# Stick-breaking attention: the softplus of the next key block is issued ahead of the sum of the present one

## The chip, the cores and the metric

The kernel runs on one core of one Trainium2 chip. The metric is the device time of one launch in microseconds (us), as the median of three runs. Engines are named as in the profile: PE is TensorE's matmul stream and PEld its weight loads, DVE is VectorE, ACT is ScalarE, POOL is GpSimd, and SP is the engine that issues most DMA transfers. Each engine takes its own instructions in the order in which they stand in its queue, and waits on semaphores for the others.

## The reference, cut to what matters

A decoder layer: an input projection, a chunked gating MLP beside stick-breaking attention (4 heads of 128, 1,024 positions), an output projection, and a mixture of 32 experts. Everything is float32. The change touches the attention alone:

```python
z = jnp.einsum('bhqd,bhkd->bhqk', qb, kf[:, :, :kl]) * scale
log_fail = jnp.where(causal, jax.nn.log_sigmoid(-z), 0.0)
within = jnp.einsum('bhqni,ij->bhqnj', log_fail, after_in_block)
later = lax.cumsum(blk, axis=3, reverse=True) - blk
log_a = jax.nn.log_sigmoid(z) + (within + later[..., None])
a = jnp.where(causal, jnp.exp(log_a), 0.0)
outs.append(jnp.einsum('bhqk,bhkd->bhqd', a, vt))
```

The key blocks of a query are swept from the last to the first, since the sum over later keys must be known before a block's weights can be formed.

## The kernel before

The attention works on key blocks of 128 (index j) against up to 512 queries at once. A `Chain` is one head and one half of the queries. Two chains of two heads run side by side, called c0 and c1 here, and a loop step k handles one key block of both. `seq` lists the 24 steps: two pairs of chains over the first half of the queries with 4 key blocks each (steps 0 to 3 and 4 to 7), and two pairs over the second half with 8 (steps 8 to 15 and 16 to 23). Because of causality the first key blocks of a pair touch 128, then 256, then 384 queries, and all others 512, so that every pair begins with widths 128, 256, 384, 512.

For one block and one head the stages are these. `z` (PE, L655) makes the scores, with a mask matmul (L659) on the diagonal. `e0`, `e1`, `e2` (ACT, L664, L669, L673) form ln(1 + exp(-|z|)) in the tile e. `sp` issues three instructions: the softplus sp = max(z, 0) + e (DVE, L681), its rounded part sh (DVE, a cast, L682), and its low part sl = sp - sh (POOL, L683). `ls` (DVE, L689) is min(z, 0) - e. `tri` (PE, L697 with sh and L698 with sl) adds the sum inside the block to the running PSUM tile cum. `add` (DVE, L702) forms ls + cum, `exp` (ACT, L713) the weights, and `av` (PE, L719) their product with the values. `comp` (PE, L708 and L709) then completes cum for the next block; it overwrites what `add` reads, so it waits for `add`.

The order is written out by hand under a manual schedule: each engine gets its instructions in the order of the loop's calls, and `each(k, f)` issues stage f for c0 and then c1. `z` and the three e stages run two steps ahead, `sp` and `ls` one step ahead. A finished pair is normalized by `fin0` to `fin5`: `fin0` in the next pair's first step, `fin1` to `fin3` in its second (PE L730, POOL L128, PE L736, DVE L740), `fin4` in its third and `fin5` (the DVE subtraction L748, called yl) in its fourth. After the attention come two transfers issued on POOL (L1076, into the tile xk that holds the keys before), and the output projection.

Of the kernel before, what the change touches and what calls it, by code (L numbers as in the profile page):

```python
# [58 lines left out]
def body(ctx, tc, A, out):  # L59
# [366 lines left out]
    def at(s, fn):  # L426
        todo.setdefault(s, []).append(fn)
# [192 lines left out]
    def wo_load(i):  # L620
        if i < 16:
            cg, b = i // 4, (i + 2) % 4
            wo_raw[i] = wr.tile([P, 2, 512], F32, name="wo")
            SY.dma_start(wo_raw[i], A["w_out"][cg, b])
# [8 lines left out]
    def ya_load(t):  # L633
        y = op.tile([P, DG], F32, name="yld")
        SY.dma_start(y, y_d[t * P:(t + 1) * P, :])
        return y

    with ExitStack() as c3:
# [113 lines left out]
        with tc.manual_schedule():  # L752
            seq = []
            for half in range(2):
                for hp2 in range(2):
                    ch = [Chain(half, 2 * hp2), Chain(half, 2 * hp2 + 1)]
                    seq += [(ch, j) for j in range((half + 1) * HT - 1, -1, -1)]
            n = len(seq)

            def each(i, f):  # L760
                if 0 <= i < n:
                    ch, j = seq[i]
                    for c in ch:
                        f(c, j)

            for i in range(2):
                wo_load(i)
            G.dma_start(wgr, A["w_gr"])
            yas = {t: ya_load(t) for t in range(2)}

            def scores(i):
                for f in (Chain.e0, Chain.e1, Chain.e2):
                    each(i, f)

            def first(i):
                return 0 <= i < n and seq[i][1] == seq[i][0][0].top

            each(0, Chain.z)
            each(1, Chain.z)
            scores(0)  # L780
            each(0, Chain.sp)
            each(0, Chain.ls)
            scores(1)
            for k in range(n + 1):
                each(k, Chain.tri)
                each(k, Chain.add)
                each(k + 2, Chain.z)
                each(k, Chain.comp)
                if 0 < k and seq[k - 1][1] == 0:
                    for i in range(6):  # L790
                        for c in seq[k - 1][0]:
                            at(k + (0, 1, 1, 1, 2, 3)[i], getattr(c, f"fin{i}"))
                if first(k - 2):
                    each(k - 2, Chain.av)
                if not first(k - 1):
                    each(k - 1, Chain.av)
                each(k + 1, Chain.sp)
                each(k + 1, Chain.ls)
                each(k + 2, Chain.e0)
                each(k, Chain.exp)  # L800
                each(k + 2, Chain.e1)
                each(k + 2, Chain.e2)
                for f in todo.pop(k, []) if k < n else ():
                    f()
            fins = [f for k in sorted(todo) for f in todo[k]]
            todo.clear()
# [710 lines left out]
```

## Time and profile before

| | |
|---|---|
| median of 3 runs | 1617.72 us (1617.65 to 1617.85) |
| profiled execution | 1615.23 us, of which span 1613.4 us |
| attention in the profiled execution | from 535.07 us (first z) to about 668 us of the span |
| mean granted TensorE clock | 0.973 of full speed |

The span is the time from the first to the last instruction of the profiled execution. The time of that execution is 1.8 us longer than its span and 2.5 us below the median of the runs, so differences are made against the execution's own time and then carried over to the median. Stretches of the trace are given as microseconds from the span's start.

### The profile page before, as it was taken

The numbers are of one execution on the slowest core, as the hardware profiler recorded it, in microseconds if no ns is written. First come the engines' busy times: TensorE is split into PE (matmuls) and PEld (weight loads), VectorE is DVE, ScalarE is ACT, GpSimd is POOL, SyncE is SP. The second block draws the span as 40 slices with busy tenths as digits, with TensorE's granted clock in tenths as the row PEclk, the third lists the DMA queues.
The fourth block names the chain that finished last, engine by engine and source line by source line (L and its number), as shares of the span: only waits on it lengthen the run. The fifth ranks groups of instructions, "written<-read, shape, count | busy, mean of one in ns | idle before, by whom it ended". The sixth has DMA issues, their size and how long they took to land.

```text
span 1613.4 us, 21346 instructions
## 1 busy us (share of the span) xinstructions
PE 1518.8 (94%) x6818; PEld 1151.6 (71%) x6818; DVE 1221.2 (76%) x2220; ACT 945.1 (59%) x2014; POOL 315.2 (20%) x288
## 2 busy tenths in 40 slices
PE   4999998999999899899999869999989999999996
PEld 4788887888888665578878656666656666666664
DVE  5889675867787588668856768887868888888883
ACT  5442588755434667432223467777767777777771
POOL 2000132010011334320001322324221212211111
PEclk8899999999999999999999979999989999999998
DMA  9987478768776000468857568999999999999972
GB/s 378 351 315 242 155 260 297 258 238 310 279 258 228 1 1 1 154 211 299 291 187 289 200 209 318 354 369 346 387 341 365 360 361 370 366 362 356 358 299 33
DMA packets 94394, 433.94 MB, mean 269 GB/s; under 512 B 13073, under 2 KB 13185, under 8 KB 64193
## 3 DMA queue, kind: packets, MB, share of 16 engines
q1 hardware_dynamic: 82000, 377.54, 63.3%
q0 software_dynamic: 11984, 52.85, 11.2%
q10 hardware_dynamic: 288, 2.10, 0.3%
q8 instruction: 56, 0.92, 0.2%
q14 instruction: 66, 0.53, 0.1%
HBM read 399.89 MB, written 43.02 MB: 275 GB/s over the span
## 4 chain that ended last, share of the span: by engine, by line
PE 40%; DMA 34%; issue 13%; DVE 5%; ACT 4%; POOL 2%; POOLq 0%; another core or an unknown queue 0%; SPq 0%; DVEq 0%; ACTq 0%
DMA out<-y,idx 22%; PE acc L322 22%; PE acc L867 9%; DMA xg<-u_d,idx 7%; DMA out<-xi 2%; DMA wm<-in_w_mod 2%; PE lg L913 1%; PE yp L719 1%; POOL sl L683 1%; PE z L655 1%; DVE macc L182 1%; DVE sp L681 1%; ACT junk L347 1%; DVE sh L682 1%; PE tr L906 1%
## 5 line engine op out<-in xcount | busy, mean ns | idle before, releaser
L1282 DVE TENSOR_TENSOR wl<-wx,wh 128x1024 fp32r<-128x1024 f32 x256 | 309.5, 1219 | 13.5 <-ACT wh L1281 12.5
L1281 ACT ACTIVATE wh<-wx 128x1024 fp32r<-128x1024 f32 x256 | 273.4, 1070 | 49.0 <-PE gu L1291 34.8
L1314 PE MATMUL dn<-wx,actT 128*128 128x512 f32 x512 | 242.4, 597 | 6.1 <-DMA wx<-in_w_down 5.5
L1291 PE MATMUL gu<-wh,xh 128*128 128x512 f32 x512 | 239.7, 468 | 0.0
L182 DVE SCALAR_TENSOR_TENSOR macc<-wm,sc_c,macc 128x512 f32<-128x512 f32 x296 | 222.2, 751 | 11.5 <-DMA wm<-in_w_mod 3.4
L322 PE MATMUL acc<-wh,hh 128*128 128x512 f32 x640 | 209.8, 398 | 3.4 <-ACT hh L278 1.8
L322 PE MATMUL acc<-wl,hh 128*128 128x512 f32 x640 | 206.7, 393 | 2.9 <-DVE wl L307 2.7
L322 PE MATMUL acc<-wh,hl 128*128 128x512 f32 x640 | 206.6, 393 | 0.4 <-DVE hl L279 0.4
L1291 PE MATMUL gu<-wl,xh 128*128 128x512 f32 x512 | 203.1, 397 | 0.1
L1291 PE MATMUL gu<-wh,xl 128*128 128x512 f32 x512 | 201.9, 394 | 0.0
L1224 POOL DMA_INDIRECT out<-y,idx x52 | 94.9, 1825 | 459.2 <-DVE y L1315 453.1
L1315 DVE TENSOR_TENSOR y<-dn,gate 128x512 f32<-128x512 f32 x128 | 88.5, 692 | 112.0 <-PE dn L1314 101.6
L867 PE MATMUL acc<-wo,yh 128*128 128x512 f32 x512 | 169.3, 412 | 0.0
L1270 ACT ACTIVATE xh<-tp,b2c 128x128 fp32r<-128x128 f32 x512 | 146.8, 383 | 17.8 <-PE tp L1265 17.7
L1314 PEld LDWEIGHTS dn<-wx,actT 128*128 128x128 f32 x512 | 96.5, 189 | 82.6 <-issue 63.1
L1272 DVE SCALAR_TENSOR_TENSOR xl<-tp,b2c,xh 128x128 fp32r<-128x128 f32 x512 | 143.5, 343 | 3.9 <-ACT xh L1270 3.9
L322 PEld LDWEIGHTS acc<-wl,hh 128*128 128x128 f32 x640 | 120.7, 189 | 30.0 <-DVE wl L307 5.0
L322 PEld LDWEIGHTS acc<-wh,hl 128*128 128x128 f32 x640 | 121.2, 189 | 26.9 <-DVE hl L279 1.1
L322 PEld LDWEIGHTS acc<-wh,hh 128*128 128x128 f32 x640 | 119.6, 190 | 27.6 <-ACT hh L278 1.9
L307 DVE TENSOR_TENSOR wl<-w,wh 128x1024 fp32r<-128x1024 f32 x80 | 97.6, 1221 | 34.2 <-ACT wh L306 34.1
L306 ACT ACTIVATE wh<-w 128x1024 fp32r<-128x1024 f32 x80 | 83.0, 1053 | 63.1 <-PE acc L322 51.6
L1291 PEld LDWEIGHTS gu<-wl,xh 128*128 128x128 f32 x512 | 97.4, 190 | 30.2 <-issue 15.1
(246 smaller groups left out, 2326.7 us busy)
## 6 DMA issues: line engine op xcount, KB each, us to landing
wx<-in_w_gu SPq DMA_DIRECT2D x128, 1024.0 KB
wm<-in_w_mod SPq DMA_DIRECT2D x160, 512.0 KB
wx<-in_w_down SPq DMA_DIRECT2D x64, 1024.0 KB
w<-in_w_in SPq DMA_DIRECT2D x80, 512.0 KB
x<-in_w_mod SPq DMA_DIRECT2D x16, 1024.0 KB
wo<-in_w_out SPq DMA_DIRECT2D x16, 512.0 KB
xi<-in_x SPq DMA_DIRECT2D x24, 256.0 KB
out<-xi SPq DMA_DIRECT2D x24, 256.0 KB
```

Source lines behind the costliest of these rows:

```text
L182: V.scalar_tensor_tensor(self.acc, t[:, j, :], sc, self.acc, op0=ALU.mult, op1=ALU.add)
L307: V.tensor_tensor(wl, w, wh.bitcast(F32), op=ALU.subtract)
L322: T.matmul(accs[t], a, b, start=(first and j == 0 and n == 0), stop=(last and j == 1 and n == 2))
L867: T.matmul(acc, y[a][:, c, ts_], w[b][:, c % 2, :], start=(n_ == 0 and i == 0), stop=(n_ == 7 and i == 2))
L1224: return G.indirect_dma_start(out=out, out_offset=bass.IndirectOffsetOnAxis(ap=idx, axis=0), in_=y, in_offset=None, bounds_check=S - 1, oo ...
L1270: SC.activation(xh[:, j, :], self.p[:, j, :], AF.Identity, bias=b2c[:, b * 4 + j:b * 4 + j + 1])
L1272: V.scalar_tensor_tensor(xl[:, j, :], self.p[:, j, :], b2c[:, b * 4 + j:b * 4 + j + 1], xh[:, j, :].bitcast(F32), op0=ALU.add, op1=ALU.sub ...
L1281: SC.activation(self.wh[q], w, AF.Copy)
L1282: low = lambda: V.tensor_tensor(self.wl[q], w, self.wh[q].bitcast(F32), op=ALU.subtract)
L1291: T.matmul(self.gu, a[c // 4][:, c % 4, :], b[q][:, k, :], start=(c == 0 and i == 0), stop=(c == 15 and i == 2))
L1314: T.matmul(d, self.aT[:, f, :], self.wd[f][:, cs], start=(f == 0), stop=(f == 1))
L1315: V.tensor_tensor(self.y[:, cs], d, gate2[:, cs], op=ALU.mult)
```

## The change

The call that issues `sp` of step k+1 moves from behind the `av` calls to between `tri` and `add` of step k. Nothing is added or removed.

```diff
             for k in range(n + 1):
                 each(k, Chain.tri)
+                each(k + 1, Chain.sp)
                 each(k, Chain.add)
                 each(k + 2, Chain.z)
                 each(k, Chain.comp)
...
                 if not first(k - 1):
                     each(k - 1, Chain.av)
-                each(k + 1, Chain.sp)
                 each(k + 1, Chain.ls)
                 each(k + 2, Chain.e0)
                 each(k, Chain.exp)
```

The order of PE, ACT and SP is the same as before. On DVE, in a full step of the last pair (512 queries wide; ls<-ls,cum is `add`, ls<-z,e is `ls`, yl is `fin5` of the pair before, - is before and + is now):

```order
 L748 TENSOR_TENSOR yl_4731<-u_5243,yh_4730 128x512
 L748 TENSOR_TENSOR yl_4731<-u_5247,yh_4730 128x512
+L681 SCALAR_TENSOR_TENSOR sp<-z,e 128x512
+L682 CAST sh<-sp 128x512
+L681 SCALAR_TENSOR_TENSOR sp<-z,e 128x512
+L682 CAST sh<-sp 128x512
 L702 TENSOR_TENSOR ls<-ls,cum 128x512 x2
-L681 SCALAR_TENSOR_TENSOR sp<-z,e 128x512
-L682 CAST sh<-sp 128x512
-L681 SCALAR_TENSOR_TENSOR sp<-z,e 128x512
-L682 CAST sh<-sp 128x512
 L689 SCALAR_TENSOR_TENSOR ls<-z,e 128x512 x2
```

The two softplus instructions and the two casts of the next step stood behind the two `add`; now they stand ahead of them.

On DVE, at the third step of a pair that follows another (384 wide; u is the output of the finished pair, L740 is its `fin3`):

```order
 L740 SCALAR_TENSOR_TENSOR u_5243<-u_5243,hcol,yp 128x512
 L740 SCALAR_TENSOR_TENSOR u_5247<-u_5247,hcol,yp 128x512
+L681 SCALAR_TENSOR_TENSOR sp<-z,e 128x512
+L682 CAST sh<-sp 128x512
+L681 SCALAR_TENSOR_TENSOR sp<-z,e 128x512
+L682 CAST sh<-sp 128x512
 L702 TENSOR_TENSOR ls<-ls,cum 128x384 x2
-L681 SCALAR_TENSOR_TENSOR sp<-z,e 128x512
-L682 CAST sh<-sp 128x512
-L681 SCALAR_TENSOR_TENSOR sp<-z,e 128x512
-L682 CAST sh<-sp 128x512
 L689 SCALAR_TENSOR_TENSOR ls<-z,e 128x512 x2
```

Here the `add` of the 384-wide block goes behind the four instructions of the 512-wide one, all of them behind `fin3`.

On POOL, at the end of the attention (sl is the low part, the DMA rows are the two transfers into the old key tile):

```order
-L683 TENSOR_TENSOR sl<-sp,sh 128x512 x6
-L1076 DMA xk<-mod_d 128x2048
-L683 TENSOR_TENSOR sl<-sp,sh 128x512 x2
-L1076 DMA xk<-mod_d 128x2048
+L683 TENSOR_TENSOR sl<-sp,sh 128x512 x8
+L1076 DMA xk<-mod_d 128x2048 x2
 L683 TENSOR_TENSOR sl<-sp,sh 128x512 x2
```

The first transfer stood ahead of the sl of step 22 and now stands behind it, beside the second.

## Rows read from the trace of the kernel before

**Rows 1.** Busy time in stretches (us: each engine's busy us, clock, DMA share, GB/s).

```profile
600.00:620.00 20.00, 17.71 (x59) 9.94 (x59) 19.13 (x30) 12.85 (x28) 8.98 (x7) 1.00 0.00 0
```

**Rows 2.** Waits in the attention, 535 to 668 us: total us, times, longest.

```profile
PE cum L698 <- POOL sl L683: 10.7, 17, 1.0
...
DVE ls L702 <- PE cum L698: 7.1, 17, 1.2
...
DVE sp L681 <- ACT e L673: 2.7, 2, 2.4
```

**Rows 3.** Timeline, DVE in a full step: start us, us, instruction, [idle before <-releaser].

```profile
607.62 0.67 DVE L702 TENSOR_TENSOR ls<-ls,cum 128x512 f32<-128x512 f32 x1
...
609.14 0.68 DVE L681 SCALAR_TENSOR_TENSOR sp<-z,e 128x512 f32<-128x512 f32 x1
...
610.92 1.11 DVE L682 CAST sh<-sp 128x512 fp32r<-128x512 f32 x1
...
611.96 1.27 DVE L689 SCALAR_TENSOR_TENSOR ls<-z,e 128x512 f32<-128x512 f32 x2
```

**Rows 4.** Timeline, ACT in the same full step.

```profile
606.23 1.14 ACT L673 ACTIVATE e<-e 128x512 f32<-128x512 f32 x2
...
610.75 1.14 ACT L713 ACTIVATE ls<-ls 128x512 f32<-128x512 f32 x2
...
612.83 1.14 ACT L673 ACTIVATE e<-e 128x512 f32<-128x512 f32 x2
```

**Rows 5.** Timeline, PE and POOL around the same full step.

```profile
601.41 0.50 PE L698 MATMUL cum<-sl,tri_r 128*128 128x512 f32 x1 [0.41 <-POOL sl L683]
...
608.00 0.50 PE L698 MATMUL cum<-sl,tri_r 128*128 128x512 f32 x1 [0.95 <-POOL sl L683]
...
609.66 0.80 PE L708 MATMUL cum<-sh,comp_r 128*128 128x512 f32 x1
...
612.20 1.29 POOL L683 TENSOR_TENSOR sl<-sp,sh 128x512 fp32r<-128x512 f32 x1 [0.45 <-DVE sh L682]
...
613.55 0.51 PE L698 MATMUL cum<-sl,tri_r 128*128 128x512 f32 x1
```

**Rows 6.** Timeline, a pair's first step (add 128, sp 256).

```profile
556.20 0.42 DVE L681 SCALAR_TENSOR_TENSOR sp<-z,e 128x256 f32<-128x256 f32 x1 [0.28 <-ACT e L673]
...
556.95 0.28 PE L708 MATMUL cum<-sh,comp_r 128*128 128x128 f32 x1
...
557.89 0.74 DVE L689 SCALAR_TENSOR_TENSOR ls<-z,e 128x256 f32<-128x256 f32 x2
```

**Rows 7.** Timeline, a pair's third step (add 384, sp 512), behind fin3.

```profile
567.67 0.75 DVE L740 SCALAR_TENSOR_TENSOR u<-u,hcol,yp 128x512 f32<-128x512 f32 x1 [0.89 <-PE yp L736]
...
569.74 0.39 PE L708 MATMUL cum<-sh,comp_r 128*128 128x384 f32 x1
...
571.62 0.58 PE L697 MATMUL cum<-sh,tri_r 128*128 128x512 f32 x1
...
573.72 0.50 PE L698 MATMUL cum<-sl,tri_r 128*128 128x512 f32 x1 [0.94 <-POOL sl L683]
```

**Rows 8.** Timeline, the first pair, steps 1 to 3.

```profile
542.67 0.93 ACT L673 ACTIVATE e<-e 128x384 f32<-128x384 f32 x2
...
546.49 0.54 DVE L702 TENSOR_TENSOR ls<-ls,cum 128x384 f32<-128x384 f32 x1
...
547.76 0.39 PE L708 MATMUL cum<-sh,comp_r 128*128 128x384 f32 x1
...
552.19 0.50 PE L698 MATMUL cum<-sl,tri_r 128*128 128x512 f32 x1 [0.95 <-POOL sl L683]
```

**Rows 9.** Busy time in two stretches behind the attention (columns as in Rows 1).

```profile
672.00:674.00 2.00, 0.00 (x0) 0.00 (x0) 1.00 (x1) 1.97 (x3) 0.00 (x0) 1.00 0.78 229
676.00:678.00 2.00, 2.00 (x9) 1.81 (x9) 1.37 (x3) 0.21 (x1) 0.38 (x1) 0.50 0.52 209
```

**Rows 10.** Timeline, DVE near the end, the cast of c1 of step 22.

```profile
655.26 1.82 DVE L682 CAST sh<-sp 128x512 fp32r<-128x512 f32 x1
```

## The prediction

> **What bounds the attention now.** I read three views. The busy time of a stretch of full steps [rows 1] shows PE at 17.71 and DVE at 19.13 of 20 us, and DMA at 0.00: both engines are nearly full, and no transfer goes on that a longer or shorter attention could hide. So a microsecond won or lost here should move all that follows by as much.
>
> The waits [rows 2] show what the change can aim at: PE waits 10.7 us for the low parts sl, and DVE 7.1 us for `tri`. They also show the other side: DVE has waited for the e stages only twice, 2.7 us in all.
>
> The timeline of a full step [rows 3 to 5] shows the ring that sets its period. From the last `tri` of one step (608.00) to that of the next (613.55) it is 5.55 us: the last low part lets `tri` run, then come the second `add`, two softplus and two casts on DVE, the low part of c1 on POOL (612.20, 1.29 long), and `tri` at 613.55. The change takes `add` out of this ring, and if nothing else closed, PE would not wait for sl any more.
>
> **What the move does.** DVE takes its instructions in order, so each `add` now waits until the four sp and sh instructions ahead of it are done. What waits for `add` is `comp` on PE, with `av` and the next `tri` queued behind it, and `exp` on ACT, with the e1 and e2 of step k+2 behind that. And e2 of step k+2 is what the next softplus waits for. A new ring closes, once around per step: exp(k), e1 and e2 (k+2), sp and sh (k+2), add(k+1), exp(k+1). Before, `add` stood ahead of the softplus, so the same dependences needed two steps per turn.
>
> In the trace the softplus has some room, but not enough. e2 of c0 is done at about 606.85 [rows 4] (606.23, and 0.62 for the first of the pair), and its softplus starts at 609.14 [rows 3], so it could go 2.3 us earlier. But softplus and casts take 609.14 to 611.96, 2.82 us. In this step `add` would start at 607.62 + 2.82 = 610.44 and end 0.67 later, at 611.1, while `comp` began at 609.66 [rows 5]: PE loses over 1 us at once.
>
> **A. Full steps.** The new ring from rows: exp to e2 2.08 us, 610.75 to 612.83 [rows 4], first e2 0.62 (four ACT instructions in 2.08 are 0.52 each, so of a pair's 1.14 the first needs 0.62), softplus and casts 2.82, `add` 0.67: 6.19. I take 6.2 with the handoffs, against 5.55. In the step that also holds yl, before 6.59, from 601.41 to 608.00 [rows 5], DVE is full in both orders: I take 6.65. In each second-half pair four steps follow a 512-wide one, one of them with yl: 3 x 0.65 + 0.06 = 2.0 us, for two pairs **+4.1**.
>
> **B. First step of a pair.** The softplus of 256 starts at 556.20, already behind a wait for e2, and its casts end at 557.89 [rows 6]. `add` of 128 then needs about 0.28 (0.67 and 0.54 for 512 and 384 [rows 3, 8], 0.13 less for each 128), so `comp` starts at 558.2 and not at 556.95. PE's queue stands 1.25 us. Three pairs follow another one in this way: **+3.8**.
>
> **C. Third step of a pair.** The second L740 ends at 568.42 [rows 7]; now 2.82 of softplus and casts and 0.54 of `add` come before `comp`, which starts at 571.78 and not at 569.74: 2.04 late. Behind it `tri` of the 512 block goes, whose last part waited 0.94 us for sl; that wait is now gone, which leaves 1.1. PE's ends are modelled, so this is an upper bound, and the lower is about 0.5 if the true wait was longer; I take 1.0. Three pairs: **+3.0**.
>
> **D. First pair.** No `fin3` stands there, so the ring itself decides. e2 of 384 is done for c0 at about 543.2 [rows 8]; softplus and casts of 384 lie halfway between 1.69 and 2.82 [rows 3, 6], 2.26, and `add` of 256 is 0.41: exp(1) at 545.9. From there exp 0.61 (ACT pairs of 256, by the steps between 0.93 and 1.14), e1 1.04, e2 0.62, softplus and casts 2.82 and `add` 0.54: `comp` of step 2 at 551.5 and not at 547.76. The way from `comp` to the last `tri` is that of C, 1.88 and 1.16 without its wait: 554.6 and not 552.19. **+2.2**, with the same caveat.
>
> **Clock.** In D PE stands still for 3.8 us. In 672 to 674 us PE did nothing, and at 676 to 678 the granted clock was 0.50, which is 1.2 of 2.4 GHz [rows 9]. Some 2.7 us of PE work (`comp`, `av`, `tri`) would then take twice as long; I count **+1.5** for the chance that the fall hits it whole.
>
> **E. End.** The cast of c1 in step 22 took 1.82 and not 1.11 [rows 3, 10], since the first transfer on POOL held up the low part of c0. The transfer now stands behind step 22: **-0.7**. Both transfers feed only the output projection behind the attention; if they came too late, its first use of the tile would wait.
>
> Nothing is added to any engine, so the costs are all order. Sum: 4.1 + 3.8 + 3.0 + 2.2 + 1.5 - 0.7 = **+13.9 us**. Against the profiled execution: 1615.2 + 13.9 = 1629.1. The median of the runs lies 2.5 above that execution, which gives **1631.6 us**, 0.9% slower.
>
> **Rivals.**
>
> *Faster: the new ring stays open.* If e2 were always done early enough, PE's 10.7 us of waiting for sl would go: 1617.7 - 10.7 = 1607.0. For it speaks that DVE hardly ever waited for e2 [rows 2]. It decides at `comp`: `add` must be done when z of step k+2 is through, so the softplus would have to move up by at least 2.82 us, and rows 3 and 4 show 2.3 of room in a step with wide blocks and none in a narrow one [rows 6]. Chance 0.07.
>
> *About even: the low parts pay for the sums.* PE's delays at `comp` and its waits at `tri` are in the same queue; if each delay took the place of a wait, the 10.7 us would be given back in full against the 13.9: +3.2, 1620.9. Against it: B has no wait for sl behind it to give back, and in A the ring does not go through sl. Chance 0.10, and half of that within the limit of no change.
>
> *Slower still: the clock falls in the new waits.* Each full step would have about 1 us of PE standing still, on top of the shorter gaps that it has. A full step at 1.2 GHz needs at least 10 us of PE: its matmuls fill about 5.3 of the 5.55 now. That is +4.4 us above 6.2 for each such step; three of them give about 1645. In 600 to 620 PE's gaps were no bar to a clock of 1.00 [rows 1], and the rows of 672 to 678 needed a gap of over 2 us. The Trainium skill (TensorE: Matmul & The Clock Gate, "HAM oscillation — how this bites in real kernels") says that bursts of matmuls with long waits between them bring the clock down again and again. By that rule the fall would come back in every step; [rows 9] agree for one long wait, and no row here shows it for short ones. Chance 0.13.
>
> **How the numbers follow.** My forecast has 0.70, with its own range 1624 to 1639: A could be +5.7 if PE's work behind `comp` adds to the ring, B to D could be half. The range of 8 in 10 reaches from 1621 (the even case) to 1643 (two or three slow-clock steps); it leaves out the faster case, the lowest even ones and the clock's tail. A change within 0.2% (3.2 us) can't be told from none here. Faster by more 0.07, within 0.07 (half the even case, the lowest of the forecast), slower 0.86.
>
> **What the profile after would show.** Right: a period of 6.2 us between the last `tri` of full steps; DVE's softplus waiting for ACT's e2 in most steps, far above 2.7 us in all; PE's wait for sl near zero, and in its place PE waiting for `add` (L702) at `comp`; the first pair's `comp` of step 2 near 551.5; the output projection beginning about 14 us later and all behind it as before. Wrong: a full step at 5.4 us or less, or `comp` that starts as soon as z is through. If the attention is longer by 14 us but the whole is not, a transfer behind it had room that I did not see.

## The result, and the profile after

The changed kernel took **1635.52 us** (median of 4 runs, 1633.39 to 1638.57) against 1617.78 us (1617.65 to 1617.90): a ratio of 1.0112, with an interval of 1.0097 to 1.0126. It is slower by 1.1%, or 17.7 us; the forecast was 13.9.

The profiled execution took 1634.69 us, with a span of 1632.8 us and a mean granted clock of 0.971. It is 19.5 us longer than the one of before. 0.7 of that lies ahead of the attention, 17.6 in it, and 1.2 behind it. The attention is measured here from the start of the last `tri` matmul (L698 of c1) of step 0 to that of step 23: 124.90 us before (539.18 to 664.08) and 142.46 after (539.86 to 682.32).

The waits of the attention, 535 to 690 us (engine, line, what it waited for: us in total, times, longest), beside [rows 2]:

```profile
PE cum L708 <- DVE ls L702: 24.3, 16, 2.6
...
ACT ls L713 <- DVE ls L702: 19.2, 15, 3.2
...
DVE sp L681 <- issue: 11.4, 8, 2.5
DVE sp L681 <- ACT e L673: 9.1, 8, 2.4
...
PE cum L698 <- POOL sl L683: 0.2, 1, 0.2
```

Read it from the bottom. The wait at which the change could aim, PE for the low parts, fell from 10.7 us to 0.2. In its place PE waits 24.3 us for `add` (L702) at `comp` (L708), ACT waits 19.2 for the same `add`, and the softplus (L681) waits 9.1 for e2. The 11.4 put down to "issue" end when e2 ends as well (the one before the softplus at 549.11 ends 0.70 after the e2 pair began at 548.41). That is a ring seen from its three engines: `add` waits for the softplus, `exp` for `add`, and the next softplus for the e2 behind `exp`.

The timeline of the full steps that answer to [rows 3 to 5] (start us, us, instruction, [idle before <-releaser]):

```profile
615.06 1.23 ACT L713 ACTIVATE ls<-ls 128x512 f32<-128x512 f32 x2 [0.54 <-DVE ls L702]
615.08 0.50 PE L708 MATMUL cum<-sh,comp_r 128*128 128x512 f32 x1 [1.20 <-DVE ls L702]
...
617.23 1.13 ACT L673 ACTIVATE e<-e 128x512 f32<-128x512 f32 x2
617.94 0.69 DVE L681 SCALAR_TENSOR_TENSOR sp<-z,e 128x512 f32<-128x512 f32 x1 [1.12 <-ACT e L673]
...
619.34 1.27 POOL L683 TENSOR_TENSOR sl<-sp,sh 128x512 fp32r<-128x512 f32 x1 [3.45 <-DVE sh L682]
...
619.87 1.02 DVE L682 CAST sh<-sp 128x512 fp32r<-128x512 f32 x1
620.81 1.27 DVE L702 TENSOR_TENSOR ls<-ls,cum 128x512 f32<-128x512 f32 x2
621.52 1.23 ACT L713 ACTIVATE ls<-ls 128x512 f32<-128x512 f32 x2
621.54 0.50 PE L708 MATMUL cum<-sh,comp_r 128*128 128x512 f32 x1 [0.76 <-DVE ls L702]
```

One turn of the ring goes from `exp` at 615.06 to `exp` at 621.52, 6.46 us: 2.17 from `exp` to e2 (617.23), 0.71 to the softplus (617.94), 2.87 for softplus and casts to `add` (620.81), 0.71 to the next `exp`. The steps before and behind are the same (608.59 to 615.06, 621.52 to 627.98). `comp` starts with the first `exp`, since both need the same `add`.

The busy time and the clock in stretches (columns as in [rows 1]):

```profile
546.00:558.00 12.00, 8.86 (x34) 7.70 (x35) 9.21 (x19) 5.17 (x14) 4.61 (x6) 0.72 0.00 1
572.00:576.00 4.00, 3.67 (x20) 3.52 (x19) 2.53 (x5) 0.56 (x2) 0.00 (x0) 0.68 0.00 0
578.00:582.00 4.00, 3.77 (x13) 3.54 (x14) 2.97 (x8) 2.83 (x8) 2.08 (x3) 0.57 0.00 0
605.00:625.00 20.00, 16.87 (x51) 8.74 (x50) 17.12 (x27) 15.00 (x27) 7.66 (x6) 1.00 0.00 0
628.00:634.00 6.00, 6.00 (x15) 3.32 (x16) 3.44 (x9) 2.01 (x6) 1.68 (x3) 0.72 0.00 1
678.00:682.00 4.00, 3.26 (x10) 1.87 (x11) 2.48 (x5) 1.23 (x2) 2.43 (x2) 1.00 0.47 181
```

In full steps (605 to 625) no engine is full any more: DVE fell from 19.13 of 20 us to 17.12. They wait for one another around the ring. PE stands still for up to 1.2 us in each step there, and the granted clock stays at 1.00. In the four stretches at 546 to 558, 572 to 582 and 628 to 634 it fell towards 0.50 (1.2 GHz). Before, the same four had 1.00; of the attention only 566 to 570 us (0.57, at the matmuls of `fin1` to `fin3`, which run at 572 to 576 after) and 586 to 590 us (0.59, and 1.00 after) were low.

PE at the places of terms D, C and A, at the last `comp` that waits for `add`, and at the first matmul of the output projection:

```profile
552.57 0.44 PE L708 MATMUL cum<-sh,comp_r 128*128 128x384 f32 x1 [2.40 <-DVE ls L702]
...
578.23 0.69 PE L708 MATMUL cum<-sh,comp_r 128*128 128x384 f32 x1 [2.56 <-DVE ls L702]
...
625.11 0.40 PE L698 MATMUL cum<-sl,tri_r 128*128 128x512 f32 x1
...
633.28 0.40 PE L698 MATMUL cum<-sl,tri_r 128*128 128x512 f32 x1
...
678.74 0.50 PE L708 MATMUL cum<-sh,comp_r 128*128 128x512 f32 x1 [2.48 <-DVE ls L702]
...
686.34 0.72 PE L867 MATMUL acc<-wo,yh 128*128 128x512 f32 x2
```

The output projection began at 668.20 before: it is 18.1 us later. The step from 625.11 to 633.28 is 8.17 us long where a full step has 6.46; the clock was at 0.72 in it (628 to 634). The wait of 2.48 us ahead of 678.74 is longer than most others, and the clock behind it stayed at 1.00 (678 to 682).

Set against each other by the same mark, the last `tri` of each step, the attention grew as follows:

| stretch (step to step) | before, us | after, us | longer by |
|---|---|---|---|
| D: first pair, 0 to 3 | 13.01 | 16.88 | 3.87 |
| B: first step of a pair, 4 to 5, 8 to 9, 16 to 17 | 4.25, 4.25, 4.20 | 5.64, 5.64, 5.22 | 3.8 (1.39, 1.39, 1.02) |
| C: third step, 6 to 7 | 5.41 | 7.81 | 2.40 (clock 0.57) |
| C: third steps, 10 to 11 and 18 to 19 | 5.50, 5.73 | 6.73, 6.72 | 2.2 |
| 9 to 10 | 9.33 (clock 0.59 at 586 to 590) | 7.53 | -1.80 |
| A: full steps 11 to 15 | 23.19 | 27.96 | 4.77 (clock 0.72 in the last) |
| A and E: full steps 19 to 23 | 23.87 | 26.27 | 2.40 |
| all others together | | | -0.1 |

### The profile page after: what moved, and what is told of

Same layout as the page of the kernel before. It is cut to its first block, busy times and chain, and to the rows that moved or that the text cites. A ratio compares the mean times of both kernels' runs of the same rounds, so it can differ in the third digit from the quotient of the medians.

```text
span 1632.8 us, 21326 instructions
## 1 busy us (share of the span) xinstructions
PE 1523.0 (93%) x6818; PEld 1154.2 (71%) x6818; DVE 1218.7 (75%) x2220; ACT 947.7 (58%) x2014; POOL 315.4 (19%) x288
## 4 chain that ended last, share of the span: by engine, by line
DMA 32%; PE 12%; issue 12%; DVE 2%; ACT 1%; POOLq 0%; POOL 0%; another core or an unknown queue 0%; DVEq 0%; ACTq 0%
DMA out<-y,idx 22%; PE acc L867 9%; DMA xg<-u_d,idx 7%; DMA out<-xi 2%; PE lg L913 1%; PE tr L906 1%; DVE sp L681 0%; DVE sh L682 0%; DVE wo L836 0%; DMA b2c<-mod_d 0%; ACT wo L835 0%; DVE xk L951 0%; DMA wo<-in_w_out 0%; ACT ls L713 0%; PE gu L1291 0%
```

## Experiments

The theory (T1) is the ring of the prediction: exp, e1 and e2, softplus and casts, `add`, once around per step. The rival (T2) is that `add` is late only because DVE has four more instructions ahead of it: then `comp` waits whatever ACT does, and the way over `exp` plays no part. The profiled execution of each kernel gives the steps; the kernel before had medians of 1617.58 us beside the first four kernels, 1616.88 beside the next four, and 1617.04 beside the last two. Ahead of the attention and behind it, where all these kernels are the same, the traces differ by up to 4 us (the first z starts at 535.2 to 538.9 us), so the steps of the attention say more than one profiled execution's whole time.

**1 and 2. The ring is cut on ACT.** In the changed kernel `exp` of step k goes behind e1 and e2 of step k+2, so that e2 no longer waits for `add`. The same edit in the kernel before is the control.

```diff
                 each(k + 2, Chain.e0)
-                each(k, Chain.exp)
                 each(k + 2, Chain.e1)
                 each(k + 2, Chain.e2)
+                each(k, Chain.exp)
```

> The changed kernel with one more move: on ACT the exp of step k is issued behind e1 and e2 of step k+2 and no longer ahead of them. Theory 1 (a ring exp, e1, e2, softplus, add, exp closes once per step): the ring is cut, since e2 no longer waits for add. What is left is the way z, e0, e1, e2, softplus, add, comp, av, tri, z, which takes two steps, about 11.4 us by the rows of before, so a full step goes from 6.46 to about 5.7 us and the time from 1635 to about 1627 us (1622 to 1630). Theory 2 (add is late only because it stands behind the four softplus and cast instructions on DVE, whatever ACT does): full steps stay at 6.4 and the time at 1635, within 3 us.

> The kernel before with the same move of exp behind e1 and e2 on ACT: the control. By theory 1 there is no ring through exp before the change, so 1617.8 us within 1.5 us; by theory 2 the same. More than 1620 would say that exp behind e2 makes av late, and that e1_exp_last carries this cost too.

Measured: 1627.23 us with the cut, ratio 1.0066 (1.0049 to 1.0083); the control 1618.07 us, ratio 1.0005 (0.9996 to 1.0015). Cutting the ring on another engine, with DVE's order as in the changed kernel, gives back 8 of its 17.7 us, and the same edit does nothing without the change. The mean granted clock over the attention is 0.94 in both traces, with the cut and without, so the gain is not the clock's. ACT in full steps of the first of the two:

```profile
608.99 1.14 ACT L713 ACTIVATE ls<-ls 128x512 f32<-128x512 f32 x2
...
613.28 1.14 ACT L673 ACTIVATE e<-e 128x512 f32<-128x512 f32 x2
614.32 1.14 ACT L713 ACTIVATE ls<-ls 128x512 f32<-128x512 f32 x2
...
620.16 1.14 ACT L673 ACTIVATE e<-e 128x512 f32<-128x512 f32 x2
...
621.20 1.14 ACT L713 ACTIVATE ls<-ls 128x512 f32<-128x512 f32 x2
```

e2 now comes ahead of `exp`, and the steps alternate: `exp` to `exp` 5.33 and 6.88, the last `tri` to the next 5.32, 6.88, 5.30, 6.29. So no ring of one step sets them. The step of 6.88 us is the one with yl, which is long in every order (6.60 before, 6.90 with the change); what makes the one of 6.29 long was not taken apart. PE still waits 16.5 us for `add` at `comp`, so T2's delay is real too. By the last `tri`, steps 11 to 15 are 23.79 us long (23.19 before, 27.96 with the change), steps 19 to 23 25.38 (23.88 and 26.27; the clock was low in the last), and the first steps of a pair 4.61, 4.61 and 4.19, so most of A and B is gone. The third steps stay at 7.79 (at a low clock, as with the change alone), 6.73 and 6.44 us. There, in term C, lies the largest part of what is left: `comp` stands behind four instructions whatever ACT does.

**3 and 4. The ring is lengthened on ACT.** Between e1 and e2 goes an instruction that only writes |e| to a tile that nobody reads, in the changed kernel and in the one before.

```diff
                 SC.activation(e, e, AF.Exp, scale=-1.0)
+                junk = at_.tile([P, 512], F32, name="junk", bufs=1)
+                SC.activation(junk[:, self.q0(j):], e, AF.Abs)
```

> The changed kernel with one ACT instruction more per head and step between e1 and e2: |e| is written to a tile that nobody reads, as wide as the step (0.52 us each at 512). Theory 1: the pair lies on the ring, so each full step gets 1.0 us longer (6.46 to 7.5), narrower ones less, some 13 us in all: 1648 us (1644 to 1653). Theory 2: ACT is busy for some 4.2 of 6.46 us in a step and can take 1.0 more, so 1635 within 3 us.

> The kernel before with the same idle ACT instruction between e1 and e2. Theory 1: e2 of c0 was done 2.3 us before its softplus began in a full step, so 1.0 us more fits there, and only narrow steps and the ends of the pairs may show it: 1617.8 us plus 0 to 3 us. If ACT were what bounds the attention, 1630 or more.

Measured: 1659.88 us in the changed kernel, ratio 1.0262 (1.0245 to 1.0280), which is 24 us above it; 1624.94 us in the kernel before, ratio 1.0049 (1.0032 to 1.0066). The direction is T1's, the size is larger than expected. The changed kernel with the idle instruction, whose lines stand two further down (L715 is `exp`, L675 e2, L683 the softplus):

```profile
628.34 1.23 ACT L715 ACTIVATE ls<-ls 128x512 f32<-128x512 f32 x2 [0.38 <-DVE ls L704]
...
631.85 1.14 ACT L675 ACTIVATE e<-e 128x512 f32<-128x512 f32 x2
...
632.56 0.69 DVE L683 SCALAR_TENSOR_TENSOR sp<-z,e 128x512 f32<-128x512 f32 x1 [2.46 <-ACT e L675]
...
636.13 1.23 ACT L715 ACTIVATE ls<-ls 128x512 f32<-128x512 f32 x2 [1.44 <-DVE ls L704]
```

From `exp` to e2 it is now 3.51 us and not 2.17, and the turn is 7.79 and not 6.46: 1.34 more work on ACT's part of the ring makes the turn 1.33 longer, one for one. The eight turns from step 10 to 14 and from 18 to 22 are each 1.25 to 1.45 us longer than in the changed kernel. In the kernel before the same work leaves a full step at 5.55 us (L700 is the last `tri`):

```profile
612.36 0.50 PE L700 MATMUL cum<-sl,tri_r 128*128 128x512 f32 x1 [0.95 <-POOL sl L685]
...
617.91 0.50 PE L700 MATMUL cum<-sl,tri_r 128*128 128x512 f32 x1
```

So ACT's way from `exp` to e2 is in the ring of the changed kernel and not in that of before. Five of its eight full steps keep their length within 0.02 us. The idle instruction cost the kernel before 7.4 us, of which its profile shows 4.6 in the attention: in narrow steps, 0.4 and 0.2 in two other full steps and 0.7 in the last. In the changed kernel those eight turns are 10.7 of the 24 us. The clock has a part in the rest, since its mean over the attention is 0.87 there and 0.94 without the idle instruction; how large a part is open.

**5 and 6. The change in one part of the steps.** The softplus goes early only in the steps ahead of which a 512-wide block is summed (k from 11 to 14 and 19 to 22, term A and E), or only in all the others (B, C, D). The edit of number 5 against the kernel before; number 6 has the two conditions exchanged:

```diff
+            def full(k):
+                return k in (11, 12, 13, 14, 19, 20, 21, 22)
...
                 each(k, Chain.tri)
+                if full(k):
+                    each(k + 1, Chain.sp)
                 each(k, Chain.add)
...
-                each(k + 1, Chain.sp)
+                if not full(k):
+                    each(k + 1, Chain.sp)
```

> The change in the eight steps alone whose block and next block are both 512 wide (steps 11 to 14 and 19 to 22); the other steps as before. Theory 1: term A alone. The rows of the changed kernel have 6.45 for 5.55 us in six of these steps and 6.9 for 6.6 in the two with yl, and give 0.7 back at the end: +5 us, 1622.8 (1620 to 1625). Rival (what costs are the narrow steps, and the full ones only pay for the clock that fell behind them): within 1.5 us of 1617.7.

> The change in all steps but those eight. Theory 1: terms B, C and D with their clock, which are the rest of +17.7: about +11 us, 1629 (1625 to 1632). With e5_full_only it should add up to the whole change within 3 us; if both together are far less than +17.7, a step pays only when its neighbour was moved too.

Measured: the full steps alone 1624.63 us, ratio 1.0051 (1.0031 to 1.0070); the others alone 1629.91 us, ratio 1.0079 (1.0057 to 1.0101). The two losses add up to 1.3% where both together cost 1.1%; in the attention of the profiles they are 5.5 and 10.3 us of the 17.6. The mean clock over the attention is 0.97 and 0.96 in the two, 0.97 before and 0.94 with the whole change, so the clock may hold the 1.8 us between, which is not shown. The last `tri` of steps 12 and 13 in number 5, and of steps 8 and 9 in number 6:

```profile
612.44 0.39 PE L698 MATMUL cum<-sl,tri_r 128*128 128x512 f32 x1
...
618.87 0.40 PE L698 MATMUL cum<-sl,tri_r 128*128 128x512 f32 x1
```

```profile
586.81 0.27 PE L698 MATMUL cum<-sl,tri_r 128*128 128x128 f32 x1
...
592.45 0.28 PE L698 MATMUL cum<-sl,tri_r 128*128 128x256 f32 x1
```

In the first, the full steps are 6.35, 6.90, 6.43, 6.47 and 6.34, 6.90, 6.45, 6.46 us long, all at a clock of 1.00 (605 to 625 and 645 to 673 us), 5.2 more than before. In the second the full steps are those of before to 0.01 us in sum, and the first steps of a pair are 1.39, 1.39 and 1.02 longer. A with E, and B, are thus each seen by themselves. C and D are not: step 6 to 7 takes 8.13 us there, with the clock in it.

**7. Filling the waits.** To see what the clock's falls cost, 16 short matmuls on constants go ahead of the scores in five steps behind which long waits stand (1.7 to 2.6 us at `comp`); the scores overwrite what they write.

```diff
+                for _ in range(self.fill):
+                    T.matmul(z[:, 0:P], tri_r, comp_r, start=True, stop=True, skip_group_check=True)
                 T.matmul(z, kT[:, h, j * P:(j + 1) * P],
...
                 each(k, Chain.add)
+                for c in seq[k + 2][0] if k + 2 < n else ():
+                    c.fill = 8 if k in (1, 2, 6, 10, 18) else 0
                 each(k + 2, Chain.z)
```

> The changed kernel with 16 short matmuls of constants (128 by 128, 0.11 us each) ahead of the scores in steps 1, 2, 6, 10 and 18, into the score tile that the scores then overwrite: work for PE in the waits for add, where the granted clock fell to 0.50 in the profile of the change (546 to 558, 572 to 582). If the clock is the part of +17.7 that the order alone (about +12 to 13) does not explain, it stays at 1.00 there and the time goes from 1635 to about 1631 (1629 to 1633). If the clock has no part in it, the 1.8 us in each of five steps lie inside the wait and the time stays at 1635 within 2, or they delay the scores and it goes up by 3 us or more.

Measured: 1637.03 us, ratio 1.0114 (1.0091 to 1.0137), no gain over the change, where about 1631 was expected if the clock was the rest of the loss. The windows of its profile:

```profile
572.00:576.00 4.00, 3.46 (x29) 3.42 (x28) 2.09 (x4) 0.98 (x2) 1.49 (x2) 1.00 0.00 0
578.00:582.00 4.00, 3.13 (x16) 2.71 (x17) 3.73 (x10) 2.95 (x9) 1.84 (x3) 1.00 0.00 0
594.00:600.00 6.00, 5.48 (x33) 5.40 (x32) 1.91 (x5) 1.83 (x4) 1.99 (x2) 0.72 0.00 0
628.00:634.00 6.00, 4.66 (x10) 2.61 (x11) 4.02 (x9) 2.03 (x6) 2.55 (x4) 0.72 0.01 1
```

At 572 to 582 us the clock stayed at 1.00, and step 6 to 7 took 6.75 us and not 7.81: 1.06 us is what the fall cost there, and 1.34 is what term C costs without it (6.75 less 5.41). But the clock fell at 594 to 600 instead, at 628 to 634 as in the changed kernel, and again near the end (0.79 at 678 to 686); over the attention its mean is 0.95, against 0.94. The fill also has a price: behind two of the filled steps, 11 to 12 and 19 to 20 are 6.95 and 6.96 us long for 6.45 and 6.46. So the fall at one place can be priced; what all of them cost together cannot be read from this run.

**8. Alternate by head.** If the wait for the low parts is to go without closing the ring, the first softplus may go ahead of the *second* `add`, but not ahead of the first. This order of DVE is `add` of c0, softplus and cast of c0, `add` of c1, softplus and cast of c1, from the kernel before:

```diff
                 each(k, Chain.tri)
-                each(k, Chain.add)
+                for c in range(2):
+                    for i, f in ((k, Chain.add), (k + 1, Chain.sp)):
+                        if i < n:
+                            f(seq[i][0][c], seq[i][1])
                 each(k + 2, Chain.z)
...
-                each(k + 1, Chain.sp)
                 each(k + 1, Chain.ls)
```

> The kernel before with another order on DVE: add of c0, softplus and cast of c0 of the next step, then add of c1, softplus and cast of c1. Theory 1: add stays ahead of the softplus of its head, so no ring through exp closes; the ring of before through the last tri, add, softplus, cast and low part loses the instructions of c0 (about 2 us), and the cast of c1 no longer waits for the low part of c0, which POOL has done by then. Full steps go to PE's own 5.3 us, those with yl from 6.6 to about 5.9: 1613.5 us (1611 to 1616). Theory 2 (every softplus ahead of an add costs): add of c1 goes behind one softplus and one cast, so 1618 to 1622.

Measured: **1611.46 us, ratio 0.9964 (0.9952 to 0.9976)**: faster than both kernels, and than the one before by 0.4%. Its waits, 535 to 668 us:

```profile
PE cum L708 <- DVE ls L702: 4.9, 8, 0.9
...
DVE sp L681 <- ACT e L673: 4.3, 4, 2.4
...
PE cum L698 <- POOL sl L683: 1.1, 3, 0.7
```

A full step of it in the timeline, DVE and POOL, and the last `tri`:

```profile
606.77 0.68 DVE L702 TENSOR_TENSOR ls<-ls,cum 128x512 f32<-128x512 f32 x1
607.03 1.30 POOL L683 TENSOR_TENSOR sl<-sp,sh 128x512 fp32r<-128x512 f32 x1 [2.31 <-DVE sh L682]
607.37 0.68 DVE L681 SCALAR_TENSOR_TENSOR sp<-z,e 128x512 f32<-128x512 f32 x1
...
608.09 0.52 DVE L682 CAST sh<-sp 128x512 fp32r<-128x512 f32 x1
608.78 1.28 POOL L683 TENSOR_TENSOR sl<-sp,sh 128x512 fp32r<-128x512 f32 x1 [0.45 <-DVE sh L682]
...
610.46 0.69 DVE L702 TENSOR_TENSOR ls<-ls,cum 128x512 f32<-128x512 f32 x1 [0.65 <-PE cum L698]
610.49 0.40 PE L698 MATMUL cum<-sl,tri_r 128*128 128x512 f32 x1
...
615.84 0.39 PE L698 MATMUL cum<-sl,tri_r 128*128 128x512 f32 x1
```

The two low parts on POOL (1.30 and 1.28 long) lie 1.75 apart (1.74 before), but the second is done at 610.06, ahead of the last `tri`, which starts at 610.49. DVE has idle time again (0.65 us for PE), and a full step takes 5.35 us (610.49 to 615.84) and not 5.55. PE is busy 18.61 of 20 us in 600 to 620 us, against 17.71 in [rows 1]. The attention is 118.97 us long, 5.9 less than before. 3.2 of that lie in the eight full steps; 1.9 lie in step 9 to 10, where the clock was low before, and are not the order's alone.

**9. The same alternation, the softplus first.** Softplus and cast of c0, `add` of c0, softplus and cast of c1, `add` of c1: only half of the softplus work stands ahead of the first `add`.

```diff
-                    for i, f in ((k, Chain.add), (k + 1, Chain.sp)):
+                    for i, f in ((k + 1, Chain.sp), (k, Chain.add)):
```

> The alternate order of e8_alternate with the two swapped: softplus and cast of c0 of the next step, add of c0, softplus and cast of c1, add of c1. Theory 1: each add again stands behind the softplus of its own head, so the ring through exp closes once per step, but with one softplus and one cast in it (about 1.1 us) and a second pair only for c1. By the rows of before: add of c0 ends, exp of c0, then exp of c1 must wait for add of c1 some 1.9 us later, e1 of both and e2 of c0 end at about 4.1, softplus, cast and add of c0 at 5.95: a full step of about 6.0 us against 6.45 of the change and 5.35 of e8_alternate, and 1623 us in all (1619 to 1627). If what counts is that the softplus comes early, it should be as fast as e8_alternate, 1611.5; if it is any softplus ahead of add, as slow as the change, 1634.

Measured: 1630.33 us, ratio 1.0084 (1.0064 to 1.0105), above the range expected. The profiled execution, whose own time was 1622.05 us, is within it, and shows the ring again on ACT:

```profile
602.97 1.29 ACT L713 ACTIVATE ls<-ls 128x512 f32<-128x512 f32 x2
...
608.85 1.30 ACT L713 ACTIVATE ls<-ls 128x512 f32<-128x512 f32 x2
```

5.88 us per turn, between 5.55 and 6.46, near the 6.0 expected. The median alone would not decide: at 1630.33 us it lies nearer to the 1634 of the rival (any softplus ahead of `add` costs as much as the change) than to 1623. It is the turn that speaks for the ring. The other three runs took 1628.91, 1631.74 and 1632.89 us, at mean granted clocks of 0.970, 0.967 and 0.967, where the profiled one had 0.976. The longer runs have the lower clock; in which steps they lost it is not in the one trace, and stays open.

**10. Is there more in number 8?** Its order with `exp` behind e2, as in number 1.

```diff
-                each(k, Chain.exp)
                 each(k + 2, Chain.e1)
                 each(k + 2, Chain.e2)
+                each(k, Chain.exp)
```

> e8_alternate with exp behind e1 and e2 on ACT. Theory 1: in e8_alternate a full step is 5.35 us, which is PE's own work, and no ring through exp is closed, so nothing is left to cut: the same as e8_alternate within 1.5 us, 1611.5 (1610 to 1613). If an ACT wait still sets the narrow steps there, 1609 or less.

Measured: 1610.61 us, ratio 0.9952 (0.9936 to 0.9968), the same as number 8 within their intervals. There is no ring over `exp` left to cut.

## Why the prediction was right, point by point

The forecast (1631.6 us, slower by 0.9%) had the sign, the mechanism and the place; its sum was 3.7 us too small in the attention. Two of its terms do not follow from their own figures: twice 2.0 is 4.0 and not 4.1 (A), and 554.6 less 552.19 is 2.4 and not 2.2 (D). Together they change the sum by 0.1.

**The ring** is shown: cut on ACT it gives half of the loss back (1), lengthened on ACT it takes the step along one for one (3), and in the kernel before the first edit changes nothing (2) and the second leaves the full step at 5.55 (4). Of the 8.9 us by which the attention of number 1 is longer than before, 4.3 lie in the third steps, where the plain delay of `comp` behind four instructions remains (term C, with a part of the clock's).

**A** was mis-sized. It was put at 6.2 us per step and measured 6.46 in the profile. Each link is a little longer than its row of before: `exp` to e2 2.17 for 2.08 (the second `exp` has to wait for the second `add`, so the pair takes 1.23 and not 1.14), e2 to the softplus 0.71 for 0.62, softplus and casts 2.87 for 2.82, `add` to `exp` 0.71 for 0.67. I had counted durations and next to nothing for the handoffs: 0.26 us per turn. The step with yl is 6.90 and not 6.65. Together A and E cost 5.2 us in number 5, and 5.5 with the whole change less the clock's 1.7 (below), where 3.4 stood in the sum.

**B** was right: 3.8 expected, 3.8 measured, in number 6 as well. **E** was right: without the change in the full steps (number 6) the step at the first transfer keeps its 6.21 us from `tri` to `tri`, and with it alone (number 5) the second pair loses 2.28 us and the first 2.96, 0.68 apart for 0.7 expected.

**C** and **D** hold the clock. D with its clock was put at 2.2 + 1.5 = 3.7 and is 3.9; `comp` of step 2 began at 552.57, or 551.9 without the later start of the attention, for 551.5. No trace has the changed order of D at full clock, so its 2.2 and the clock's 1.5 cannot be told apart. C was put at 1.0 each and is 1.23 and 0.99 in the two later pairs; in the second pair it is 2.40, of which number 7 shows 1.06 to be the clock.

**The clock** was counted once (1.5 us, in D) and fell at other places too. Beyond D it took about 1.1 us at step 6 to 7 and 1.7 at step 14 to 15 (8.17 us, where number 5 has 6.47 for the same step at full clock). It gave back most of the 1.8 us at step 9 to 10, where it had been low before: number 2, whose DVE and PE orders are those of before, takes 7.79 us there at full clock. Counting these 1.8 as the clock's, the difference of the sum is: A and E 2.1, C 0.6 at full clock, D 0.2, the clock 0.9 net, and -0.1 elsewhere, together 3.7. The clock's places moved again in number 7, and number 2 has none in its whole attention (mean 1.00) where the kernel before has two, so the clock's part holds for this execution and not for each.

**The rivals.** *Faster: the new ring stays open* failed where the prediction placed it: `comp` waits for `add`. *About even* is answered by the two waits: PE's wait for the low parts was given back as a whole (10.5 us), but 24.1 us came at `comp`. *Slower still* happened at single places only. With waits of up to 1.2 us at `comp` in every step, 605 to 625 us went at 1.00. Around the waits of 2.40 and 2.56 us the clock was 0.72 and 0.57, but it stayed at 1.00 behind the one of 2.48 us ahead of 678.74, and the step behind the wait of 1.87 us at 628.00 went at a low clock here and at 1.00 in number 5, where the same wait is 1.88 us. So the length of a wait does not tell here whether the clock falls. The rule of the Trainium skill (TensorE: Matmul & The Clock Gate, "HAM oscillation — how this bites in real kernels") says that bursts of matmuls with long waits between them bring the clock down again and again. The three longest waits here, behind one of which the clock stayed up, do not settle it, and the fall in every step that the rival had by it did not come.

## What to carry to other kernels

Before a stage is moved ahead of a waiting one in an in-order queue, follow the dependences around all engines and count how many steps one turn takes: here the move made a turn of one step out of a turn of two, and the wait that it removed was small against that. Add the handoffs to the durations, since they count once per link and turn. Where two independent chains share the queue, interleaving them (one chain's critical stage, its next stage, then the other chain) can hide the same latency without closing the ring.

## What the runs showed of the hardware

The cast (L682) of the same shape takes 0.43 us when POOL is idle and 1.02 to 1.11 us when it starts beside POOL's subtraction ([rows 3]; 1.02 at 619.87 here), and 0.52 in number 8, where the subtraction of the other chain is about to end. Its end follows the end of the subtraction and not its own start: it comes 0.28 us behind it in all three (612.03 behind 611.75 before, 620.89 behind 620.61 after, 608.61 behind 608.33 in number 8), and 0.28 or 0.29 behind it for every 512-wide cast of the second chain in these three traces. The cast of 1.82 us in [rows 10] fits this too: it ends at 657.08, behind a subtraction that ended at 656.79. The Trainium skill (GPSIMD Engine Reference, "1. Specifications") says that POOL shares its SBUF interfaces with VectorE, with contention for some of VectorE's instructions; the trace agrees, and puts it at up to 0.7 us per cast. Number 8's order draws the second cast out from under most of the subtraction, 0.6 us in a full step; how much of its gain is this, and how much the order of `add`, was not measured apart.

The clock's falls wander: filling one wait kept the clock up there and it fell in later stretches (number 7), and the traces of the kernel before and of number 2, with the same order on PE and DVE, have a mean clock of 0.97 and 1.00 over the attention. Four runs of one kernel (number 9) lay between 1622 and 1633 us with mean clocks from 0.976 down to 0.967.
